# A state-space layer beside attention: the causal mask once per group, the sigmoid's linear part on ScalarE, chunk-end decays from the middle's, step sums later

## The chip, the cores and the metric

The kernel runs on one core of a Trainium2 chip. A core has a matrix engine (TensorE, in the profile PE for its matmuls and PEld for its weight loads), a vector engine (VectorE, DVE), an engine for functions of one input (ScalarE, ACT), a general engine (GpSimd, POOL) and SyncE (SP), whose queue issues most of the weight loads. Each engine works through its own queue in order; semaphores hold an instruction until its inputs are there. The metric is the device time of one execution in microseconds, the median of several runs.

## The reference

Input `x` has 256 positions of 1024 numbers. Two layers follow each other, then a norm over the 1024 columns.

The first layer projects the normed `x` into eight parts: a gate `z`, the state-space inputs `xs`, `B`, `C`, the step sizes `dt`, and `q`, `k`, `v`, a gate rank and an output gate for gated linear attention.

The state-space half: a causal convolution of width 4 and silu over `xs`, `B`, `C`; then for 16 heads in two groups, with `a_cs` the running sum of `dt * a`,

```python
decay_ij = jnp.exp(jnp.where(causal, a_cs_i - a_cs_j, -jnp.inf))
cb = jnp.einsum('bcign,bcjgn->bcgij', c_c, b_c)          # one per group
y_diag = einsum(cb * decay_ij, x * dt)                   # one per head
```

The linear attention half, in chunks of 64 positions, with `gcs` the running sum of `log_sigmoid(gate) / 16` within a chunk and `ref` its value in the chunk's middle (position 32):

```python
scores = einsum(q * exp(gcs - ref), k * exp(ref - gcs))  # within a chunk, causal
chunk_kv = einsum(k * exp(g_last - gcs), v)              # what a chunk leaves behind
o_inter = einsum(q * exp(gcs), prev_states)              # what a chunk takes over
```

Both halves are normed, gated and projected back. The second layer is softmax attention over 16 heads with its own projections.

## The kernel before

The sequence has 256 positions, so a tile of 128 partitions by 256 columns holds one block of 128 features for all positions. Weights come in pieces of 416 or 512 KB through SP's queue; `split` (L73 to L78) makes a high part of each piece on ScalarE (L76) and the rest on VectorE (L77), and every projection is three matmuls per 128 input features: high by high, high by rest, rest by high (`mm3`, L166). In the profile `pb` is the PSUM tile of the projections by block of features, `pa` of those by position, `h_b`, `l_b`, `h_a`, `l_a` the two parts of their weights.

TensorE's order is written out by the program itself. A planner (L129 to L153) keeps a clock of its own, `clock["now"]`, to which each matmul adds a price (L155 to L160: 106.7 ns for the 128 x 256 matmul of a projection). Small tasks are generators: each does a step and then yields a number of ns, and `due()` runs after each `mm3` the steps whose time has come. The numbers are in `DL` (L26 to L28). So a larger number puts more projection matmuls ahead of a step. VectorE, ScalarE and GpSimd are not ordered by hand except at the very start: the scheduler of the language takes, engine by engine, what is ready in its own model of time, earlier lines of the program first. The resulting queues are fixed in the program.

The main loop (L610 to L625) goes through `ORDER_A`: blocks 8 and 9 (`B`, `C`), 10 to 17 (`q` and `k`), 0 to 7 (`xs`) and the position-wise projections `a2` to `a4`, mixed. Around it run these tasks:

- `co_first` (L360): from the first projections the step sizes `dt` and `dta`, a chain of some dozen small VectorE instructions that ends at L388; then after `gt` the transposed gate rank, after `ac` the matmuls `acp` (L397, running sums of `dta`), after `act` their transpose and, in two steps `lg`, the gate products (`lg`, L412). From each, `gab` = |g + b| on ScalarE (L416) and `gmn` = min(g + b, 0) on VectorE (L417); then Exp and Ln over `gab`, which need two tables, their difference (L422) and the running sum `gcs` within each chunk (L423).
- `co_conv` (L435), one per block 0 to 9: `pad`, a scaling on ScalarE, three VectorE instructions `cu` (L444), a Tanh and the product `xs` or `bc` (L448).
- `co_cb` (L457): the products `cb` of `C` and `B`, one per group, copied to `cbT` (L465).
- `co_pair` (L468), one per block 0 to 7, two heads: the transpose `xtp` of `xs`, its product with `dt` (`xdt`), the decays `e` (Relu and Exp on ScalarE, L481 to L485), the causal mask on them by GpSimd (L487, one select per head over two 128 x 128 parts), the product with `cbT` (L489) and the matmuls `yp`.
- `co_gla_qk` (L508): from `gcs` the four decay tiles `e1` to `e4` and their products with `q` or `k` (L517 to L528), and the tiles `qs`, `ks` (L533 to L536). `co_gla_pair` (L541) uses them in the score matmuls `gs` and the outputs `go`.

After these come the second half of the first layer (`pc`), the attention layer (`pv`, `pp`, `as`, `ptp`, `ao`) and the last projection (`pf`).

Of the kernel before, what the change touches and what calls it, by code (L numbers as in the profile page):

```python
# [9 lines left out]
F32 = mybir.dt.float32  # L10
F32R = mybir.dt.float32r
AF = mybir.ActivationFunctionType
ALU = mybir.AluOpType
AX = mybir.AxisListType

P = 128
T = 256
# [5 lines left out]
NWARM = 20  # L23
AHEAD = 4

DL = {"rb": 1300, "gt": 1500, "ac": 7300, "act": 2600, "lg": 2150, "ln": 2250, "cb": 12400,  # L26
      "pair0": 11900, "pair1": 9700, "gla0": 650, "glagap": 3650, "gla1": 3350, "gla2": 8700, "r2": 10000,
      "turn": 4150, "rb1": 4000, "at0": 2600, "at2": 5000, "at1": 3700, "at3": 1800, "gqk": 250}  # L28

# [6 lines left out]
C_CW, C_CB, C_GB, C_DS, C_GN = 24, 64, 74, 78, 86  # L36
# [8 lines left out]
def trunk(ctx, tc, xT_d, x_d, cst_d, mat_d, gw2_d, fn_d, wa_d, wb_d, wc_d, wv_d, wp_d, wf_d, out_d):  # L45
    nc = tc.nc
    V, S, G, TE = nc.vector, nc.scalar, nc.gpsimd, nc.tensor

    cpool = ctx.enter_context(tc.tile_pool(name="consts", bufs=1))
# [5 lines left out]
    sm = ctx.enter_context(tc.tile_pool(name="sm", bufs=2))  # L55
# [125 lines left out]
    cst = cpool.tile([P, C_N], F32, name="cst")  # L181
# [178 lines left out]
    def co_first(ps):  # L360
        rcol = env["rcol"]
        V.tensor_scalar(rhalf, rcol, 0.5, None, op0=ALU.mult)
        V.tensor_tensor(rsq, rcol, rcol, op=ALU.mult)
        V.tensor_scalar(rsv, rsq, 1.0 / P, None, op0=ALU.mult)
        V.tensor_scalar(rsh, rsq, 0.5, None, op0=ALU.mult)
        V.tensor_scalar(cwh, cst[:, C_CW:C_CW + 50], 0.5, None, op0=ALU.mult)
        S.activation(ea, cst[:, C_AL:C_AL + 16], AF.Exp)
        for c in range(2):
            for tt in range(2):
                tm_evac(c, tt, ps[c][tt])  # L370
        env["a1"] = True
        yield DL["rb"]
        S.activation(rb, row_bcast([rcol[:, tt:tt + 1] for tt in range(2)], "rbp")[:, 0:T], AF.Copy)
        env["rb"] = True

        V.scalar_tensor_tensor(na, dtr, -1.0, dtr, op0=ALU.mult, op1=ALU.min)
        S.activation(se, na, AF.Exp)
        V.tensor_scalar(sd, se, 2.0, None, op0=ALU.add)
        V.reciprocal(sd, sd)
        V.tensor_tensor(s1, se, sd, op=ALU.mult)  # L380
        V.tensor_tensor(s2, s1, s1, op=ALU.mult)
        V.tensor_scalar(sp, s2, 1.0 / 17, None, op0=ALU.mult)
        for q_ in (15, 13, 11, 9, 7, 5, 3):
            V.scalar_tensor_tensor(sp, sp, 1.0 / q_, s2, op0=ALU.add, op1=ALU.mult)
        V.scalar_tensor_tensor(sp, sp, 1.0, s1, op0=ALU.add, op1=ALU.mult)
        V.tensor_scalar(mx, dtr, 0.0, None, op0=ALU.max)
        V.scalar_tensor_tensor(dt, sp, 2.0, mx, op0=ALU.mult, op1=ALU.add)
        V.scalar_tensor_tensor(dta, dt, -1.0, ea[:, None, :].to_broadcast([P, 2, 16]), op0=ALU.mult, op1=ALU.mult)  # L388
        yield DL["gt"]
        gtp = pm("gtp")  # L390
        for tt in range(2):
            tr(gtp[0:16, tt * P:tt * P + P], glr[:, tt, :])
        V.tensor_copy(glT, gtp[0:16, 0:T])
        yield DL["ac"]
        acp = pm("acp")
        for tt in range(2):
            mm(acp[0:16, tt * P:tt * P + P], dta[:, tt, :], tri[tt])  # L397
        V.tensor_copy(acT, acp[0:16, 0:T])
        S.activation(ahl[0:16, :], acp[0:16, 0:T], AF.Copy)
        V.tensor_sub(ahl[32:48, :], acT, ahl[0:16, :].bitcast(F32))  # L400
        V.tensor_copy(sel, mat[:, M_SEL:M_SEL + 16])
        yield DL["act"]
        act = pm("act")
        for tt in range(2):
            TE.transpose(act[:, 16 * tt:16 * tt + 16], acT[:, tt * P:tt * P + P], ident[0:16, 0:16])
        V.tensor_copy(acs, act[:, 0:32].rearrange("p (a b) -> p a b", a=2))

        for b2 in range(2):
            lg = pm(f"lg{b2}")
            for j in range(2):  # L410
                b = 2 * b2 + j
                mm(lg[:, j * T:j * T + T], gw2[:, b * P:b * P + P], glT)  # L412
            for j in range(2):
                b = 2 * b2 + j
                gbc = cst[:, C_GB + b:C_GB + b + 1]
                S.activation(gab[:, b, :], lg[:, j * T:j * T + T], AF.Abs, bias=gbc)  # L416
                V.tensor_scalar(gmn[:, b, :], lg[:, j * T:j * T + T], gbc, 0.0, op0=ALU.add, op1=ALU.min)  # L417
            yield DL["lg"]
        S.activation(gab, gab, AF.Exp, scale=-1.0)
        S.activation(gab, gab, AF.Ln, bias=1.0)  # L420
        yield DL["ln"]
        V.tensor_sub(gmn, gmn, gab)  # L422
        V.tensor_tensor_scan(flat(gcs), flat(scanm), flat(gmn), 0.0, op0=ALU.mult, op1=ALU.add)  # L423
        env["gcs"] = True


# [30 lines left out]
    def co_cb():  # L457
        yield DL["cb"]
        for g in range(2):
            r = slice(64 * g, 64 * g + 64)  # L460
            ps = pm(f"cb{g}")
            mm(ps[:, 0:T], bc[r, 0, 0:P], bc[r, 1, :])
            mm(ps[:, T:T + P], bc[r, 0, P:T], bc[r, 1, P:T])
            sb = big.tile([P, 3 * P], F32, name=f"cbT{g}", tag=f"cbT{g}")
            S.activation(sb, ps[:, 0:3 * P], AF.Copy)  # L465
            cbT.append(sb)

    def co_pair(blk):  # L468
        yield DL["pair0"]
        tp = pm(f"xtp{blk}")  # L470
        for tt in range(2):
            tr(tp[:, tt * P:tt * P + P], xs[:, blk, tt * P:tt * P + P])
        xdt = tmp.tile([P, 2, 2, 64], F32, name=f"xdt{blk}", tag="t1c")
        V.tensor_tensor(xdt, tp[:, 0:T].rearrange("p (a b c) -> p a b c", a=2, b=2),
                        dt[:, :, 2 * blk:2 * blk + 2][:, :, :, None].to_broadcast([P, 2, 2, 64]), op=ALU.mult)
        e = tmp.tile([P, 2, 3, P], F32, name=f"e{blk}", tag="t3")
        for j in range(2):
            h = 2 * blk + j
            ab = pm(f"ab{h}")
            mm(ab[:, 0:T], sel[:, h:h + 1].to_broadcast([P, P]), ahl)  # L480
            S.activation(e[:, j, 0:2, :].rearrange("p a b -> p (a b)"), ab[:, 0:T], AF.Relu, scale=-1.0,  # L481
                         bias=acs[:, 0, h:h + 1])
            S.activation(e[:, j, 2, :], ab[:, P:T], AF.Relu, scale=-1.0, bias=acs[:, 1, h:h + 1])
        ef = e.rearrange("p a b c -> p (a b c)")
        S.activation(ef, ef, AF.Exp, scale=-1.0)  # L485
        for j in range(2):
            G.affine_select(out=e[:, j, 0:3:2, :], in_=e[:, j, 0:3:2, :], pattern=[[0, 2], [1, P]],  # L487
                            compare_op=ALU.is_ge, fill=0.0, base=0, channel_multiplier=-1)
        V.tensor_tensor(e, e, cbT[blk // 4].rearrange("p (a b) -> p a b", a=3)[:, None, :, :].to_broadcast([P, 2, 3, P]),  # L489
                        op=ALU.mult)  # L490
        yield DL["pair1"]
        yp = pm(f"yp{blk}")
        rows = [slice(64 * j, 64 * j + 64) for j in range(2)]
        for j, r in enumerate(rows):
            mm(yp[r, 0:T], xdt[:, 0, j, :], e[:, j, 0:2, :].rearrange("p a b -> p (a b)"), True, False)
        for j, r in enumerate(rows):
            mm(yp[r, P:T], xdt[:, 1, j, :], e[:, j, 2, :], False, True)
        V.scalar_tensor_tensor(y[:, blk, :], xs[:, blk, :], cst[:, C_DS + blk:C_DS + blk + 1], yp[:, 0:T],
                               op0=ALU.mult, op1=ALU.add)
# [8 lines left out]
    def co_gla_qk():  # L508
# [5 lines left out]
        e3 = big.tile([P, 16, 64], F32, name="e3", tag="s3")  # L514
        e4 = big.tile([P, 16, 64], F32, name="e4", tag="s4")
        dl = cpool.tile([P, 4, 4], F32, name="dl")
        V.tensor_tensor(e2, gcs, gcs[:, :, 32:33].to_broadcast(full), op=ALU.subtract)  # L517
        V.tensor_tensor(e4, gcs[:, :, 63:64].to_broadcast(full), gcs, op=ALU.subtract)
        S.activation(e1, e2, AF.Exp, scale=1.0 / 16)
        S.activation(e2, e2, AF.Exp, scale=-1.0 / 16)  # L520
        S.activation(e3, gcs, AF.Exp, scale=1.0 / 16)
        S.activation(e4, e4, AF.Exp, scale=1.0 / 16)
        S.activation(dl.rearrange("p a b -> p (a b)"), gcs[:, :, 63], AF.Exp, scale=1.0 / 16)
        env["gla"] = (e1, e2, e3, e4, dl)
        V.scalar_tensor_tensor(e1, qf, 0.125, e1, op0=ALU.mult, op1=ALU.mult)
        V.scalar_tensor_tensor(e3, qf, 0.125, e3, op0=ALU.mult, op1=ALU.mult)
        V.tensor_tensor(e2, kf, e2, op=ALU.mult)
        V.tensor_tensor(e4, kf, e4, op=ALU.mult)  # L528
        qs = big.tile([P, 4, 2, 64], F32, name="qs", tag="qs")
        ks = big.tile([P, 4, 2, 64], F32, name="ks", tag="ks")  # L530
        e3v = e3.rearrange("p (a c) d -> p a c d", a=4)
# [417 lines left out]
```

## Time and profile before

| | |
|---|---|
| median of 3 runs | 344.76 us (344.56 to 344.84) |
| profiled execution, its own time | 343.5 us |
| its span, first to last instruction | 341.8 us |
| busy: TensorE, VectorE, ScalarE, GpSimd | 330.9, 260.6, 235.0, 38.1 us |
| granted TensorE clock, mean | 0.996 of full |

Every row below is from that one profiled execution; times are us from the span's start unless they are marked ns. Columns of the views, from the left:

- waits: the instruction that stood, what released it, us in total, how many times, the longest
- chain: start, length, engine, what (rows overlap less than the instructions do, since each counts from the end of the one before)
- stretches: the stretch, its length, then for each engine named in the group's line its busy time and, in brackets, its instructions; then the granted clock, the share of the DMA engines and GB/s
- time line: start, length, engine, line, operation, what it writes and reads, shapes, count; in square brackets the idle time of its engine just before, and who ended it
- groups: line, engine, operation, tiles, shapes, count; busy us and mean ns of one; idle us before and what ended it

### The profile page before, as it was taken

How to read it: one execution, taken by the hardware profiler on the slowest of the kernel's cores; microseconds unless marked ns; L12 is line 12 of the kernel's file. 1: busy time of each engine (PE TensorE's matmuls, PEld its weight loads, DVE VectorE, ACT ScalarE, POOL GpSimd, SP SyncE). 2: the span in 40 equal slices, each digit the busy share in tenths (PEclk: the TensorE clock that was granted, in tenths of full speed). 3: DMA queues.
4: the chain of work that ended last, by engine and by line, in shares of the span. 5: the costliest groups of instructions: out<-in, count | busy, mean ns of one | idle time of the engine just before them, and what ended most of it. 6: DMA issues, size and time to landing. Idle time of an engine off the chain costs nothing.

```text
span 341.8 us, 5949 instructions
## 1 busy us (share of the span) xinstructions
PE 330.9 (97%) x2160; PEld 294.2 (86%) x2160; DVE 260.6 (76%) x538; ACT 235.0 (69%) x495; POOL 38.1 (11%) x56
## 2 busy tenths in 40 slices
PE   7999799999999999999999999999999999999992
PEld 7999789999888899999888888888888888888782
DVE  3978987998999767889975756557869689596552
ACT  4858669897567847768442766565797886987531
POOL 1000000223311241434300000000000000000000
PEclk9999999999999999999999999999999999999998
DMA  7995772454157834621687436637607327070003
GB/s 221 333 334 185 239 257 61 110 166 150 51 151 233 297 122 153 221 81 46 196 281 256 145 123 231 226 132 256 185 5 245 125 99 261 12 245 3 0 2 123
DMA packets 18094, 56.07 MB, mean 164 GB/s; under 512 B 2048, under 2 KB 5120, under 8 KB 17936
## 3 DMA queue, kind: packets, MB, share of 16 engines
q1 hardware_dynamic: 17344, 53.53, 48.3%
q10 hardware_dynamic: 720, 2.16, 1.8%
q8 instruction: 17, 0.28, 0.3%
q14 instruction: 13, 0.11, 0.1%
HBM read 54.63 MB, written 1.05 MB: 163 GB/s over the span
## 4 chain that ended last, share of the span: by engine, by line
PE 67%; DVE 5%; issue 2%; POOL 0%; ACT 0%; POOLq 0%
PE pp L159 20%; PE pc L159 13%; PE pb L159 7%; PE pv L159 6%; PE pa L159 6%; PE pf L159 4%; PE ao L159 2%; PE go L159 2%; PE as L159 2%; PE gs L159 2%; PE ptp L163 2%; DVE cu L444 1%; PE yp L159 1%; DVE l_a L77 1%; PE obt L163 1%
## 5 line engine op out<-in xcount | busy, mean ns | idle before, releaser
L159 PE MATMUL pb<-hh,h_b 128*128 128x256 f32 x416 | 76.9, 286 | 0.0
L159 PE MATMUL pp<-h,h_p 128*128 128x512 f32 x192 | 67.6, 402 | 0.0
L159 PEld LDWEIGHTS pb<-hh,h_b 128*128 128x128 f32 x416 | 64.6, 191 | 1.4 <-issue 0.9
L159 PE MATMUL pb<-hh,l_b 128*128 128x256 f32 x208 | 58.7, 282 | 0.0
L159 PE MATMUL pp<-h,l_p 128*128 128x256 f32 x192 | 49.9, 280 | 0.0
L159 PE MATMUL pa<-h_a,hh 128*128 128x416 f32 x160 | 42.6, 357 | 1.0 <-ACT h_a L76 1.0
L159 PEld LDWEIGHTS pp<-h,h_p 128*128 128x128 f32 x192 | 34.5, 188 | 7.0 <-issue 0.5
L159 PEld LDWEIGHTS pb<-hh,l_b 128*128 128x128 f32 x208 | 39.7, 191 | 0.0
L159 PEld LDWEIGHTS pp<-h,l_p 128*128 128x128 f32 x192 | 36.2, 189 | 2.2
L77 DVE TENSOR_TENSOR l_p<-r_p,h_p 128x1024 fp32r<-128x1024 f32 x24 | 29.2, 1222 | 8.9 <-ACT h_p L76 8.0
L77 DVE TENSOR_TENSOR l_b<-r_b,h_b 128x1024 fp32r<-128x1024 f32 x26 | 31.5, 1212 | 1.7 <-ACT h_b L76 1.5
L76 ACT ACTIVATE h_b<-r_b 128x1024 fp32r<-128x1024 f32 x26 | 27.1, 1060 | 7.1 <-DMA r_b<-in_wb 6.5
L159 PEld LDWEIGHTS pa<-h_a,hh 128*128 128x128 f32 x160 | 29.8, 188 | 2.5 <-ACT h_a L76 1.3
L76 ACT ACTIVATE h_p<-r_p 128x1024 fp32r<-128x1024 f32 x24 | 25.1, 1056 | 1.7 <-PE pv L159 1.6
L159 PE MATMUL pa<-l_a,hh 128*128 128x416 f32 x80 | 24.9, 351 | 0.0
L77 DVE TENSOR_TENSOR l_c<-r_c,h_c 128x1024 fp32r<-128x1024 f32 x16 | 19.9, 1251 | 5.4 <-ACT h_c L76 5.4
L76 ACT ACTIVATE h_c<-r_c 128x1024 fp32r<-128x1024 f32 x16 | 16.9, 1055 | 10.1 <-DMA r_c<-in_wc 8.8
L77 DVE TENSOR_TENSOR l_a<-r_a,h_a 128x832 fp32r<-128x832 f32 (+1 forms) x21 | 20.6, 986 | 2.5 <-ACT h_a L76 2.5
L76 ACT ACTIVATE h_a<-r_a 128x832 fp32r<-128x832 f32 (+1 forms) x21 | 18.1, 862 | 6.1 <-DMA r_a<-in_wa 5.9
L159 PE MATMUL pv<-h_v,h 128*128 128x512 f32 x64 | 20.1, 391 | 0.0
L487 POOL TENSOR_SCALAR_AFFINE_SELECT e<-e 128x256 f32<-128x256 f32 x16 | 11.6, 749 | 73.3 <-ACT e L485 59.4
L764 ACT ACTIVATE pt<-pt,nm 128x128 f32<-128x128 f32 (+1 forms) x32 | 14.2, 444 | 5.6 <-DVE nm L762 5.6
(234 smaller groups left out, 715.3 us busy)
## 6 DMA issues: line engine op xcount, KB each, us to landing
r_b<-in_wb SPq DMA_DIRECT2D x26, 512.0 KB, 4.2
r_p<-in_wp SPq DMA_DIRECT2D x24, 512.0 KB, 4.2
r_c<-in_wc SPq DMA_DIRECT2D x16, 512.0 KB, 4.0
r_a<-in_wa SPq DMA_DIRECT2D x19, 416.0 KB, 3.9
r_v<-in_wv SPq DMA_DIRECT2D x8, 512.0 KB, 4.4
r_f<-in_wf SPq DMA_DIRECT2D x8, 512.0 KB, 3.9
xT<-in_xT SPq DMA_DIRECT2D x8, 128.0 KB, 4.8
x<-in_x ACTq DMA_DIRECT2D x1, 1024.0 KB, 6.1
```

The lines of the kernel that those rows point to most:

```text
L76: S.activation(hi, raw, AF.Copy)
L77: V.tensor_sub(lo, raw, hi.bitcast(F32))
L159: TE.matmul(out, lhsT, rhs, start=start, stop=stop)
L163: TE.transpose(out, in_, ident)
L444: V.scalar_tensor_tensor(u, pd[:, 1 + i:1 + i + T], w(i), u, op0=ALU.mult, op1=ALU.add)
L487: G.affine_select(out=e[:, j, 0:3:2, :], in_=e[:, j, 0:3:2, :], pattern=[[0, 2], [1, P]], compare_op=ALU.is_ge, fill=0.0, base=0, channel_ ...
L764: S.activation(pt[:, cs], pt[:, cs], AF.Exp, scale=-1.0, bias=nm[:, tt:tt + 1], accum_out=sme[:, tt:tt + 1])
```

## The change

`ac` grows from 7300 to 10000, so `acp` and what hangs on it in `co_first` stand later in TensorE's order. The four `min(g + b, 0)` on VectorE become four `Relu(-(g + b))` on ScalarE, with the sign turned in the two instructions that follow. The mask goes from the decays of each head to `cbT`, once per group. In `co_gla_qk` the tiles `e3` and `e4` are no longer made by Exp from their own differences: `e3` is the finished `e1` times `exp(ref)`, `e4` the finished `e2` times `exp(g_last - ref)`, one factor per chunk and feature, and only for the three chunks each that are read.

```diff
-DL = {"rb": 1300, "gt": 1500, "ac": 7300, "act": 2600, ...
+DL = {"rb": 1300, "gt": 1500, "ac": 10000, "act": 2600, ...
...
+        gbn = sm.tile([P, 4], F32, name="gbn", tag="gbn", bufs=1)
+        V.tensor_scalar(gbn, cst[:, C_GB:C_GB + 4], -1.0, None, op0=ALU.mult)
...
-                V.tensor_scalar(gmn[:, b, :], lg[:, j * T:j * T + T], gbc, 0.0, op0=ALU.add, op1=ALU.min)
+                S.activation(gmn[:, b, :], lg[:, j * T:j * T + T], AF.Relu, scale=-1.0, bias=gbn[:, b:b + 1])
...
-        V.tensor_sub(gmn, gmn, gab)
-        V.tensor_tensor_scan(flat(gcs), flat(scanm), flat(gmn), 0.0, op0=ALU.mult, op1=ALU.add)
+        V.tensor_tensor(gmn, gmn, gab, op=ALU.add)
+        V.tensor_tensor_scan(flat(gcs), flat(scanm), flat(gmn), 0.0, op0=ALU.mult, op1=ALU.subtract)
...
             S.activation(sb, ps[:, 0:3 * P], AF.Copy)
+            diag = sb.rearrange("p (a b) -> p a b", a=3)[:, 0:3:2, :]
+            G.affine_select(out=diag, in_=diag, pattern=[[0, 2], [1, P]],
+                            compare_op=ALU.is_ge, fill=0.0, base=0, channel_multiplier=-1)
...
-        for j in range(2):
-            G.affine_select(out=e[:, j, 0:3:2, :], in_=e[:, j, 0:3:2, :], pattern=[[0, 2], [1, P]],
-                            compare_op=ALU.is_ge, fill=0.0, base=0, channel_multiplier=-1)
...
+        V.tensor_tensor(fl(dr), gcs[:, :, 63], gcs[:, :, 32], op=ALU.subtract)
         V.tensor_tensor(e2, gcs, gcs[:, :, 32:33].to_broadcast(full), op=ALU.subtract)
-        V.tensor_tensor(e4, gcs[:, :, 63:64].to_broadcast(full), gcs, op=ALU.subtract)
         S.activation(e1, e2, AF.Exp, scale=1.0 / 16)
         S.activation(e2, e2, AF.Exp, scale=-1.0 / 16)
-        S.activation(e3, gcs, AF.Exp, scale=1.0 / 16)
-        S.activation(e4, e4, AF.Exp, scale=1.0 / 16)
-        S.activation(dl.rearrange("p a b -> p (a b)"), gcs[:, :, 63], AF.Exp, scale=1.0 / 16)
+        S.activation(fl(dl), gcs[:, :, 63], AF.Exp, scale=1.0 / 16)
+        S.activation(fl(dm), gcs[:, :, 32], AF.Exp, scale=1.0 / 16)
+        S.activation(fl(dr), fl(dr), AF.Exp, scale=1.0 / 16)
         V.scalar_tensor_tensor(e1, qf, 0.125, e1, op0=ALU.mult, op1=ALU.mult)
-        V.scalar_tensor_tensor(e3, qf, 0.125, e3, op0=ALU.mult, op1=ALU.mult)
         V.tensor_tensor(e2, kf, e2, op=ALU.mult)
-        V.tensor_tensor(e4, kf, e4, op=ALU.mult)
+        V.tensor_tensor(f4(e3)[:, :, 1:4, :], f4(e1)[:, :, 1:4, :], dm[:, :, 1:4, None].to_broadcast([P, 4, 3, 64]),
+                        op=ALU.mult)
+        V.tensor_tensor(f4(e4)[:, :, 0:3, :], f4(e2)[:, :, 0:3, :], dr[:, :, 0:3, None].to_broadcast([P, 4, 3, 64]),
+                        op=ALU.mult)
```

## Rows read from the trace of the kernel before

**Rows 1.** The page: span, and busy us of each engine

```profile
span 341.8 us, 5949 instructions
...
PE 330.9 (97%) x2160; PEld 294.2 (86%) x2160; DVE 260.6 (76%) x538; ACT 235.0 (69%) x495; POOL 38.1 (11%) x56
```

**Rows 2.** TensorE's waits (PE), whole span

```profile
PE acp L159 <- DVE dta L388: 2.1, 1, 2.1
PE warmp L177 <- DVE mhalf L203: 1.3, 1, 1.3
PE pa L159 <- ACT h_a L76: 1.0, 1, 1.0
PE xtp L163 <- DVE xs L448: 0.2, 1, 0.2
```

**Rows 3.** Chain of waits, 85 us to the end

```profile
91.87 0.33 DVE ks L535
...
98.68 0.35 DVE xs L448
...
99.07 0.44 PE xtp L163 x2
...
99.74 2.15 PE pb L159 x18
...
114.59 1.64 PE gs L159 x20
```

**Rows 4.** Stretch 58.40 to 99.10 us: PE, PEld, DVE, ACT, POOL

```profile
58.40:99.10 40.70, 40.49 (x311) 37.46 (x309) 38.37 (x64) 31.47 (x59) 11.12 (x14) 1.00 0.39 112
```

**Rows 5.** VectorE's waits, 58 to 100 us

```profile
DVE e L489 <- POOL e L487: 2.3, 3, 1.0
```

**Rows 6.** Time line around `acp` and `act`

```profile
39.79 0.17 DVE L388 SCALAR_TENSOR_TENSOR dta<-dt,ea 128x32 f32<-128x32 f32 x1
...
40.02 0.61 PE L159 MATMUL acp<-mat,dta 128*16 128x128 f32 x4 [2.11 <-DVE dta L388]
...
43.99 0.29 PE L405 MATMUL act<-mat,acT 16*128 16x16 f32 x2
```

**Rows 7.** Stretch 40.50 to 43.98 us, instructions of `pb`: PE, PEld, DVE, ACT

```profile
40.50:43.98 3.48, 3.42 (x27) 3.30 (x27) 0.42 (x1) 0.00 (x0) 1.00 0.84 226
```

**Rows 8.** Groups by form, 40 to 115 us

```profile
L487 POOL TENSOR_SCALAR_AFFINE_SELECT e<-e 128x256 f32<-128x256 f32 x14 | 10.9, 797 | 62.9 <-ACT e L485 49.0 <-DVE pad L439 7.2 <-issue 6.7
...
L489 DVE TENSOR_TENSOR e<-e,cbT 128x768 f32<-128x768 f32 x7 | 6.7, 952 | 3.0 <-POOL e L487 3.0
...
L417 DVE TENSOR_SCALAR gmn<-lg,cst 128x256 f32<-128x256 f32 x4 | 1.9, 479 | 0.5 <-ACT gab L416 0.5
L416 ACT ACTIVATE gab<-lg,cst 128x256 f32<-128x256 f32 x4 | 1.9, 476 | 1.1 <-DVE gmn L417 0.9
...
L518 DVE TENSOR_TENSOR e<-gcs 128x1024 f32<-128x1024 f32 x1 | 1.2, 1211 | 0.0
...
L521 ACT ACTIVATE e<-gcs 128x1024 f32<-128x1024 f32 x1 | 1.1, 1062 | 0.0
```

**Rows 9.** Time line around `cbT` and block 1's `xs` and `xtp`

```profile
49.89 0.87 ACT L465 ACTIVATE cbT<-cb 128x384 f32<-128x384 f32 x2 [0.37 <-PE cb L159]
...
63.20 0.42 DVE L448 SCALAR_TENSOR_TENSOR xs<-cth,cu 128x256 f32<-128x256 f32 x1
64.28 0.96 DVE L489 TENSOR_TENSOR e<-e,cbT 128x768 f32<-128x768 f32 x1 [0.66 <-POOL e L487]
...
65.83 0.38 PE L163 MATMUL xtp<-mat,xs 128*128 128x128 f32 x2
```

**Rows 10.** Time line of ScalarE around Ln

```profile
52.23 1.28 ACT L420 ACT_TABLE_LOAD   x1
53.53 1.06 ACT L420 ACTIVATE gab<-gab 128x1024 f32<-128x1024 f32 x1
...
58.64 1.28 ACT L521 ACT_TABLE_LOAD   x1
```

More of the change, by code (lines that the diff above doesn't have):

```diff
@@ L24 @@
 AHEAD = 4
-DL = {"rb": 1300, "gt": 1500, "ac": 7300, "act": 2600, "lg": 2150, "ln": 2250, "cb": 12400,
+DL = {"rb": 1300, "gt": 1500, "ac": 10000, "act": 2600, "lg": 2150, "ln": 2250, "cb": 12400,
       "pair0": 11900, "pair1": 9700, "gla0": 650, "glagap": 3650, "gla1": 3350, "gla2": 8700, "r2": 10000,
@@ L516, in co_gla_qk @@
         dl = cpool.tile([P, 4, 4], F32, name="dl")
+        dr = cpool.tile([P, 4, 4], F32, name="dr")
+        dm = cpool.tile([P, 4, 4], F32, name="dm")
+        fl = lambda a: a.rearrange("p a b -> p (a b)")
+        f4 = lambda a: a.rearrange("p (a c) d -> p a c d", a=4)
+        V.tensor_tensor(fl(dr), gcs[:, :, 63], gcs[:, :, 32], op=ALU.subtract)
         V.tensor_tensor(e2, gcs, gcs[:, :, 32:33].to_broadcast(full), op=ALU.subtract)
-        V.tensor_tensor(e4, gcs[:, :, 63:64].to_broadcast(full), gcs, op=ALU.subtract)
         S.activation(e1, e2, AF.Exp, scale=1.0 / 16)
         S.activation(e2, e2, AF.Exp, scale=-1.0 / 16)
-        S.activation(e3, gcs, AF.Exp, scale=1.0 / 16)
-        S.activation(e4, e4, AF.Exp, scale=1.0 / 16)
-        S.activation(dl.rearrange("p a b -> p (a b)"), gcs[:, :, 63], AF.Exp, scale=1.0 / 16)
+        S.activation(fl(dl), gcs[:, :, 63], AF.Exp, scale=1.0 / 16)
+        S.activation(fl(dm), gcs[:, :, 32], AF.Exp, scale=1.0 / 16)
+        S.activation(fl(dr), fl(dr), AF.Exp, scale=1.0 / 16)
         env["gla"] = (e1, e2, e3, e4, dl)
         V.scalar_tensor_tensor(e1, qf, 0.125, e1, op0=ALU.mult, op1=ALU.mult)
-        V.scalar_tensor_tensor(e3, qf, 0.125, e3, op0=ALU.mult, op1=ALU.mult)
         V.tensor_tensor(e2, kf, e2, op=ALU.mult)
-        V.tensor_tensor(e4, kf, e4, op=ALU.mult)
+        V.tensor_tensor(f4(e3)[:, :, 1:4, :], f4(e1)[:, :, 1:4, :], dm[:, :, 1:4, None].to_broadcast([P, 4, 3, 64]),
+                        op=ALU.mult)
+        V.tensor_tensor(f4(e4)[:, :, 0:3, :], f4(e2)[:, :, 0:3, :], dr[:, :, 0:3, None].to_broadcast([P, 4, 3, 64]),
+                        op=ALU.mult)
         qs = big.tile([P, 4, 2, 64], F32, name="qs", tag="qs")
```

## The prediction

> **What bounds the kernel now.** I read the page's busy times first, then TensorE's waits, then the chain, then the stretches that these pointed at. The page gives TensorE 330.9 of 341.8 us [rows 1]. A modelled busy time alone proves little, so the second view decides: all the time in which TensorE stood waiting is four rows, 4.6 us together [rows 2]. Two of them (1.3 and 1.0 us) lie at the very start, before the first weights are split, and no edit touches them. The third is the one to look at: 2.11 us in which the matmuls `acp`, the running sums of the step sizes, wait for `dta` from VectorE. The fourth is 0.2 us before an `xtp`, a transpose that waits for a convolution block `xs`. So the kernel is bound by the order and amount of TensorE's work, and only what removes or adds a TensorE wait moves the end.
>
> That fourth row is small but tells of a second limit. The chain of waits enters TensorE at 99.07 us, at that `xtp`, straight from VectorE [rows 3]; ahead of it VectorE was busy 38.37 of 40.70 us from 58.40 to 99.10 [rows 4], and the missing 2.3 us are three waits of the decay product (L489) for GpSimd's mask [rows 5]. So around 99 us VectorE delivers just in time: if TensorE comes earlier, VectorE must come earlier too, or the gain is handed back there.
>
> The sum below is made against the profiled execution, 343.5 us with a span of 341.8; the median of the runs shown is 344.76, which is 1.26 more. I add that at the end.
>
> **The change, part by part.**
>
> *The step sums later (`ac` 7300 to 10000).* TensorE's order is written out by the planner. It lets a due step in after each group of three matmuls, which it charges 3 x 106.7 = 320 ns (L160). 2700 ns more are 8.4, thus 9 groups: 27 matmuls of the projection are put ahead of `acp`. In the trace 18 of them take 2.15 us [rows 3], 27 take 3.2 us; the stretch between `acp` and the next step, `act`, holds just 27, from 40.02 + 0.61 = 40.6 to 43.99 us [rows 6, 7]. Without its wait TensorE would have begun `acp` at 40.02 - 2.11 = 37.91; now it comes there at 37.91 + 3.2 = 41.1. `dta` ends at 39.79 + 0.17 = 39.96 [rows 6], and nothing ahead of it on VectorE is changed except one tiny negation (`gbn`, at the 0.17 us of `dta`). That leaves 1.0 us, so I take the whole wait as gone: -2.11 us. Bounds: 0 (if `dta` comes later by more than 1.0 + 2.1 us) to -2.11. No DMA is moved: splits and weight loads are issued by the projection blocks, whose order stays. What hangs on `acp` (its transpose, the gate products, the gate's scan) comes 3.2 - 2.1 = 1.1 us later on the clock.
>
> *Relu on ScalarE for min on VectorE.* Four VectorE instructions of 0.48 us go, four ScalarE ones of the same shape as the Abs (0.48 us) come [rows 8]: 1.9 us from one engine to the other, off TensorE. Abs and min took turns on one bank of PSUM, with waits for each other in either direction; both now stand in one queue. ScalarE waits for `gbn`, which needs only a constant.
> The Trainium skill ("ScalarE: Activation LUTs", Rules for kernel authors) says to give relu, min and add to VectorE instead. For these fp32 blocks out of PSUM the trace does not bear it out: 479 ns on VectorE, 476 on ScalarE [rows 8]. Were the rule right, the swap would cost ScalarE more than VectorE wins, and still no TensorE time.
>
> *Scan.* The subtraction before the scan becomes an addition and the scan adds the opposite sign: same shapes, 0 either way.
>
> *Chunk-end decays from the middle's.* VectorE loses one difference and two full products of 1024 columns, three instructions of 1.21 us (L518; L526 and L528 like it): -3.63 us. It gains two products of 768 columns; the nearest row is the 768-column decay product with a broadcast operand, 0.95 us [rows 8], so +1.9 (bounds: three quarters of 1.21, thus 0.91, and 1.21 each), and a 16-column difference, +0.17. ScalarE loses two Exp of 1.06 [rows 8] and gains two of 16 columns, which cannot be longer than the 0.48 of 256 columns; with the four Relu its balance is between -0.2 and +0.8 us, beside 235 us of work in a span of 342 [rows 1]. In series the new products come later, since `e3` waits for the finished `e1`. That is hidden: the last of the old ones, `ks`, ends at 92.2 and the first score matmul `gs` that reads them comes at 114.6 [rows 3], 22 us later. What the new products may wait for is ScalarE's small Exp; behind them in VectorE's queue stand convolutions. In the trace VectorE's only waits between 58 and 100 us were for GpSimd [rows 5], none for the old Exp, so I price this at 0 and keep the three-wait total of 2.3 us as its upper end.
>
> *Mask once per group.* GpSimd loses 16 selects of about 0.8 us [rows 8] and gets two. The first product that needs the masked `cbT` starts at 64.28; the copy is done at 50.76 [rows 9]. Two selects fit there many times, so the added wait costs nothing. What goes is VectorE's 2.3 us of standing before L489 [rows 5] and up to two selects of latency ahead of each `yp`.
>
> *VectorE's ledger up to 99 us*, which decides whether the gain lives: -3.63 + 1.9 + 0.17 - 2.3 = -3.9 us. To serve TensorE 2.11 us earlier, and without today's 0.24, it must gain 2.35. That leaves 1.5 us, and the 1.9 us of min removed before 52 us are not counted.
>
> **The sum:** 343.5 - 2.1 = 341.4 for the profiled execution; with 1.26 added, 342.6 us. Behind the `xtp` at 99 us TensorE has no wait at all [rows 2], so I let the rest shift as a whole.
>
> **Rivals.**
>
> *Part of the gain comes back at the second `xtp`.* The gate chain (Exp, Ln, scan) comes 1.1 us later on the clock. Convolution block 1 shares its queues; its `xs` ends at 63.62 and its `xtp` starts at 65.83 [rows 9], which becomes 63.72. If the block is late by the same 1.1 us, TensorE stands 64.72 - 63.72 = 1.0 us, and the gain is 1.1: 343.7. For it: VectorE is without a gap there. Against it: VectorE has 1.9 us less to do ahead of it.
>
> *VectorE keeps its clock.* The scheduler re-plans VectorE's queue for the whole program; if the saved time is filled by weight splits that could have waited, `xs` still ends at 99.03 [rows 3] and TensorE waits there 0.24 + 2.11 us. The profile then shows an `acp` without a wait and the same span: 344.8. The same end comes if the sums are moved but `dta` comes later too, so that the change does not do what it says.
>
> *Slower: the logarithm lands ahead of block 1's Tanh.* The ScalarE queue swaps its tables for Ln and back: a load of 1.28, Ln itself about 1.06 like the other 1024-column functions, another load of 1.28 [rows 8, 10]: 3.62 us in which no Tanh can run. Today it begins at 52.23, ahead of the block's work. Moved against the blocks by 3.2 us of TensorE work it may stand right ahead of the Tanh. Then `xs` of block 1 ends at 63.62 + 3.62 = 67.24 where TensorE is ready at 63.72; it waits 3.52, less the 2.11 won: +1.4 us, 346.2. It decides once this `xs` ends later than 65.83, today's start of its `xtp`. For it: both loads are needed in any order. Against it: the Exp of L521, 1.06 us of that queue, is gone.
> The same page of the Trainium skill (What ACT_TABLE_LOAD costs) adds a drain of 1.38 us to each load. The trace shows none: Ln's load starts at 52.23 and Ln at 53.53 [rows 10]. By the page this rival would end near 349.0.
>
> **How the numbers follow.** About 0.2%, 0.7 us, is what a measurement of this kernel can tell from no change. The forecast, 342.6, gets 0.58, with its own range of 341.9 to 343.3. Part back: 0.16, around 343.7, nearly all of it still faster by more than 0.7. VectorE keeps its clock: 0.12, no change. Slower: 0.14, from 345.5 to 346.5 or beyond, other orders of the queues that end late among them. Faster 0.73, the same 0.13, slower 0.14. The range reaches from 341.8, where no wait but those of the start is left and a little noise is added, over no change to 345.2, and leaves out most of the slower case.
>
> **What would show it.** Right: TensorE's waits hold no `acp` row and no `xtp` row above 0.3 us; `dta` still ends near 40 us and `acp` starts near 41.1; VectorE shows no wait for GpSimd before L489; `gs` starts near 112.4; the span is near 339.7. Wrong: an `acp` wait that is left (`dta` moved too), a wait of 1 us or more at an `xtp` (block 1 or the one at 97 us), or a `yp` or `gs` that waits for a product behind ScalarE's Exp. The forecast fails if any of these waits passes 1.4 us, for then less than 0.7 us of the gain remains.

## The result, and the profile after

The changed kernel takes 340.93 us (median of 4, 340.65 to 341.28) against 344.66 us of the kernel before: a ratio of 0.9895, 95% interval 0.9873 to 0.9917, so 3.7 us (2.9 to 4.4) faster. The forecast was 342.6 and its range began at 341.8: right in direction, too small by 1.7 us.

The page of the changed kernel, span and busy times, answers to [rows 1]:

```profile
span 338.9 us, 5921 instructions
...
PE 331.0 (98%) x2160; PEld 295.0 (87%) x2160; DVE 257.1 (76%) x535; ACT 234.8 (69%) x499; POOL 29.7 (9%) x42
```

TensorE has the same work, 331.0 against 330.9 us, in 2.9 us less of span. All its waits, against the four of [rows 2]:

```profile
PE warmp L177 <- DVE mhalf L203: 1.3, 1, 1.3
```

Only the unavoidable one at the start is left. Those for `acp` and for the `xtp` are gone, as forecast; the 1.0 us for the first weights is a matter of the single execution (the traces below show between 0 and 0.9 us there). The time line around `acp` answers to [rows 6]:

```profile
39.29 0.17 DVE L388 SCALAR_TENSOR_TENSOR dta<-dt,ea 128x32 f32<-128x32 f32 x1
...
40.57 0.61 PE L159 MATMUL acp<-mat,dta 128*16 128x128 f32 x4
...
44.53 0.29 PE L405 MATMUL act<-mat,acT 16*128 16x16 f32 x2
```

`dta` ends at 39.46 and `acp` starts at 40.57, 1.1 us behind it; 1.0 was forecast. In the chain of waits, `acp` now stands between projection matmuls that follow each other without a gap:

```profile
1.25 4.64 PE warmp L177 x20
...
29.14 11.50 PE pb L159 x96
40.64 0.54 PE acp L159 x4
41.19 3.42 PE pb L159 x27
```

VectorE between 58.40 and 99.10 us ([rows 4]; after the stretch and its length come PE, PEld, DVE, ACT, POOL, then the granted clock), and the 3.3 us behind `acp`, which the experiments come back to:

```profile
58.40:99.10 40.70, 40.70 (x313) 38.02 (x312) 39.75 (x66) 34.35 (x67) 3.21 (x2) 1.00 0.47 136
41.10:44.40 3.30, 3.30 (x28) 3.29 (x27) 2.83 (x6) 2.75 (x5) 0.00 (x0) 1.00 0.92 284
```

VectorE's waits from 58 to 100 us; the three for GpSimd of [rows 5] are gone:

```profile
DVE gs L273 <- ACT gth L272: 0.5, 1, 0.5
DVE xs L450 <- ACT cth L448: 0.2, 1, 0.2
DVE l_b L77 <- ACT h_b L76: 0.2, 1, 0.2
```

The new operations by form, answering to [rows 8]:

```profile
L419 ACT ACTIVATE gmn<-lg,gbn 128x256 f32<-128x256 f32 x4 | 1.9, 474 | 0.0
...
L470 POOL TENSOR_SCALAR_AFFINE_SELECT cbT<-cbT 128x256 f32<-128x256 f32 x2 | 1.2, 628 | 24.9 <-ACT cbT L467 24.9
...
L536 DVE TENSOR_TENSOR e<-e,dm 128x768 f32<-128x768 f32 x1 | 0.9, 950 | 0.0
L538 DVE TENSOR_TENSOR e<-e,dr 128x768 f32<-128x768 f32 x1 | 0.9, 944 | 0.0
```

The Relu takes the 0.47 us of the Abs beside it, the two products 0.95 and 0.94 us (forecast 0.95), the two selects on `cbT` 0.63 us each (the forecast went by the 0.8 us of the selects on the decays).

The two kernels' profiled executions are 343.5 and 340.65 us, 2.85 apart. 2.11 and 0.24 of that are the two waits, and 0.5 stands at the start (the first `pb` comes at 24.88 instead of 25.38 us). So the profiles account for the forecast's sum and for nothing of the additional gain: the medians lie 3.73 apart. What the median of before holds and its profiled execution doesn't is the first question of the experiments.

### The profile page after: what moved, and what is told of

The parts are those of the page before. It is cut to its first block, busy times and chain, and to the rows that moved or that the text cites. A ratio compares the mean times of both kernels' runs of the same rounds, so it can differ in the third digit from the quotient of the medians.

```text
span 338.9 us, 5921 instructions
## 1 busy us (share of the span) xinstructions
PE 331.0 (98%) x2160; PEld 295.0 (87%) x2160; DVE 257.1 (76%) x535; ACT 234.8 (69%) x499; POOL 29.7 (9%) x42
## 4 chain that ended last, share of the span: by engine, by line
PE 96%; issue 2%; DVE 1%; ACT 0%; POOLq 0%; POOL 0%
PE pb L159 22%; PE pp L159 20%; PE pa L159 14%; PE pc L159 13%; PE pv L159 6%; PE pf L159 5%; PE yp L159 2%; PE ao L159 2%; PE go L159 2%; PE as L159 2%; PE gs L159 2%; PE ptp L163 2%; PE warmp L177 1%; PE obt L163 1%; PE lg L159 1%
## 5 line engine op out<-in xcount | busy, mean ns | idle before, releaser
L446 DVE SCALAR_TENSOR_TENSOR cu<-pad,cwh,cu 128x256 f32<-128x256 f32 x30 | 14.4, 481 | 1.3 <-ACT cu L444 1.2
```

Source lines behind the costliest of these rows:

```text
L446: V.scalar_tensor_tensor(u, pd[:, 1 + i:1 + i + T], w(i), u, op0=ALU.mult, op1=ALU.add)
```

## The experiments

Every kernel was timed beside the kernel before, in three groups, each on a chip of its own; the median of before was 344.55, 344.59 and 344.86 us there. Theories and rivals are named A to H in the recorded expectations; where a letter comes back in a later run it has the sense that this run's text gives it.

**What a second trace of before shows.** No edit.

> The kernel before once more, for a second trace of it and for what two equal programs differ by. The forecast added 1.26 us to the profiled execution (343.5 against a median of 344.76) as if that were constant. Theory A with waits that vary: an execution near 344.7 shows more TensorE wait than the 4.6 us of the first trace, by about 1.2 us, at acp (its dta stands in VectorE's queue behind weight splits that wait for their loads) or at an xtp. Rival, the start: the additional 1.2 us stands before 26 us, in the waits for the first weights, and the acp wait is again 2.1. Rival, neither: same waits, and the difference lies outside the span. Timed against before: within 0.2%.

Measured: 344.05 (12 executions from 343.21 to 345.65), ratio 0.9995 (0.9977 to 1.0013); the traced execution took 344.73. TensorE's waits are those of [rows 2] but for the start: `acp` 2.1, `xtp` 0.2, no `pa`. The time line of its TensorE:

```profile
39.80 0.61 PE L159 MATMUL acp<-mat,dta 128*16 128x128 f32 x4 [2.09 <-DVE dta L388]
...
45.25 0.29 PE L405 MATMUL act<-mat,acT 16*128 16x16 f32 x2
```

From `acp` to `act` it needs 45.25 - 39.80 = 5.45 us, in the first trace 43.99 - 40.02 = 3.97 [rows 6], for the same 27 matmuls [rows 7]. The stretches show why (the third number from the right is the granted clock):

```profile
40.00:41.00 1.00, 1.00 (x9) 0.78 (x8) 1.00 (x2) 0.30 (x1) 0.00 (x0) 1.00 0.62 152
...
41.02:44.43 3.41, 3.41 (x18) 3.41 (x17) 2.08 (x4) 1.32 (x2) 0.00 (x0) 0.50 0.82 270
44.43:48.00 3.57, 3.57 (x27) 3.04 (x26) 3.35 (x8) 2.46 (x5) 0.00 (x0) 1.00 0.67 247
```

Behind the wait, which ends at 39.80, `acp` and the first projection matmuls still run at full clock. From 41.02 us on, 1.2 us behind the wait's end, the granted clock is 0.50 for 3.41 us, that is 1.2 instead of 2.4 GHz, and 18 matmuls go through where 28 do in the first trace, in nearly the same stretch at full clock:

```profile
41.10:44.40 3.30, 3.30 (x28) 3.17 (x27) 3.24 (x6) 2.08 (x3) 0.00 (x0) 1.00 0.90 272
```

So neither longer waits nor the start nor the time outside the span: a fourth cause that no theory had. It costs 5.45 - 3.97 = 1.48 us. Of the 52 executions of before beside the experiments, 14 took 343.0 to 343.9 us and 38 took 344.1 or more (of the twelve here, six each); the first profile, at 343.5, was of the shorter kind. The mean granted clock that is recorded with each execution fits: 0.995 to 0.997 in the 14, 0.991 to 0.994 in 37 of the 38 (the one of 344.14 us has 0.997), and 3.41 us at half clock are 0.005 of such a span. It is a hint and no proof, since this mean also counts what falls after the last matmul, where it costs nothing (in the first trace the clock is 0.50 from 340 us on, and the last matmul ends at 335.5).

**The wait filled with work.** This tells a clock that falls because TensorE stands from one that falls at this place for another reason.

```diff
-        acp = pm("acp")
+        acp = pm("acp"); [TE.matmul(acp[:, T:2 * T], hhi[:, 0, 0:P], hhi[:, 0, :], start=True, stop=True) for _ in range(16)]
```

> The kernel before with 16 matmuls of no use (128x256, into the unused half of acp's own bank) just ahead of acp, so that TensorE works through the 1.9 us that it otherwise stands; the queues of the other engines are unchanged in order. Seen so far: in two of three traces with the acp wait of 2.1 us the granted clock is at its lower level for 3.41 us right behind it, and these executions are about 1.2 us longer than the one without. Theory D (clock): it is standing still that lets the clock fall; with the wait filled the clock stays at the upper level in every execution and the time is that of the faster executions of before, 343.2 to 343.7 median, 0.8 to 1.3 us under the median of before, though the 2.1 us are as lost as ever. Rival E (the lower clock comes from something else at that place, such as acp's narrow matmuls or the loads): the clock still falls in most executions and the median stays within 0.4 us of before. Rival F (the start): the two groups of times come from the first weights, and the median stays as before.

Measured: 343.43, ratio 0.9972 (0.9960 to 0.9983); nine of ten executions took 343.0 to 343.7, the tenth 344.51. The mean granted clock is 0.995 to 0.998 in all ten, so the tenth is not late by the clock. The 16 matmuls fill the wait to 0.19 us, and the clock behind stays up:

```profile
37.62 2.08 PE L395 MATMUL acp<-hh 128*128 128x256 f32 x16
39.89 0.61 PE L159 MATMUL acp<-mat,dta 128*16 128x128 f32 x4 [0.19 <-DVE dta L388]
```

```profile
41.10:44.40 3.30, 3.30 (x28) 3.14 (x27) 3.18 (x6) 2.03 (x4) 0.00 (x0) 1.00 0.85 256
```

`acp` comes no earlier (39.89) and nothing else is changed, yet about 1.2 us of the median go: theory D, with rivals E and F out. What the matmuls of no use do is to leave only the shorter kind of execution; the 2.1 us themselves stay lost.

**Half the wait.** `ac` at 8300 in the changed kernel.

```diff
-DL = {"rb": 1300, "gt": 1500, "ac": 10000, "act": 2600, ...
+DL = {"rb": 1300, "gt": 1500, "ac": 8300, "act": 2600, ...
```

> The changed kernel with the delay ahead of acp at 8300: 6 groups of three matmuls, 2.15 us, earlier than in the changed kernel, where dta is 1.1 us ahead of acp. So acp should wait about 1.0 us. If the cost of a wait is its length alone: 1.0 us above the changed kernel, 341.9 to 342.1. Theory D with a clock that falls after any wait: another 1.2 to 1.7 us in most executions, 343.1 to 343.7, and the clock at its lower level behind acp in the trace. Theory D with a clock that falls only after a wait long enough: as by length alone, with the clock at its upper level.

Measured: 342.03, ratio 0.9929 (0.9913 to 0.9944), all five executions from 341.81 to 342.32. TensorE's waits, and the stretch behind `acp`:

```profile
PE warmp L177 <- DVE mhalf L203: 1.3, 1, 1.3
PE acp L159 <- DVE dta L388: 1.0, 1, 1.0
PE pa L159 <- ACT h_a L76: 0.9, 1, 0.9
```

```profile
41.10:44.40 3.30, 3.30 (x27) 3.10 (x26) 2.71 (x5) 2.27 (x3) 0.00 (x0) 1.00 0.95 292
```

The wait is 1.0 us, the kernel 1.1 us slower than the changed one, and the clock stays at the upper level in this trace: here the wait cost its length.

**The early sums in the changed kernel.** `ac` back to 7300, the three other edits kept.

```diff
-DL = {"rb": 1300, "gt": 1500, "ac": 10000, "act": 2600, ...
+DL = {"rb": 1300, "gt": 1500, "ac": 7300, "act": 2600, ...
```

> The changed kernel with the delay ahead of acp set back from 10000 to 7300, all else as changed. Theory A: the acp wait is back with 2.0 to 2.6 us, the xtp wait stays at 0, so it is slower than the changed kernel by 2.0 to 2.6 us and ahead of before by 0.2 us plus what differs from run to run. Theory B: equal to before, 344.7. Theory C: ahead of before by 1.3 to 1.7 us, with an acp wait of 2.1.

Measured: 344.34, ratio 0.9993 (0.9976 to 1.0010). As theory B has it, equal to before, and 3.4 us above the changed kernel: 2.1 us of wait, and in the traced execution (344.86) the granted clock is 0.50 from 41.4 to 44.8 us.

```profile
PE acp L159 <- DVE dta L388: 2.1, 1, 2.1
PE warmp L177 <- DVE mhalf L203: 1.3, 1, 1.3
```

```profile
41.40:44.75 3.35, 3.35 (x18) 3.35 (x17) 1.95 (x4) 1.24 (x3) 0.00 (x0) 0.50 0.82 291
```

The `xtp` wait is gone with the lightened VectorE, but that is 0.2 us. Without the later sums nothing is gained.

**The later sums alone.** The kernel before with `ac` at 10000; run twice.

```diff
-DL = {"rb": 1300, "gt": 1500, "ac": 7300, "act": 2600, ...
+DL = {"rb": 1300, "gt": 1500, "ac": 10000, "act": 2600, ...
```

> The kernel before with one number changed: the delay ahead of acp is 10000 instead of 7300. Theory A (the forecast's): TensorE's waits decide, and VectorE has no time to spare at 99 us. The acp wait of 2.1 us goes, but VectorE's queue is otherwise unchanged, so most of it comes back as a wait for xs at the xtp of the sixth or seventh block: a wait of 1 to 2.4 us there, and a gain over before of 0 to 1.2 us. Theory B (the later step alone is the change, VectorE's relief is idle time off the path): the whole gain of 3.7 us, near 341.0, and no xtp wait above 0.3 us. Theory C (the relief of VectorE and GpSimd is worth about 1.5 us by itself, the acp wait 2.1): a gain of 2.0 to 2.4 us, no xtp wait above 0.3 us.

> The later step sums alone once more, for a second trace. Its first profiled execution was 341.57, with a gs wait of 1.1 us, though the median was 342.48. If the wait varies with the loads: 1.1 to 2.5 us at gs in this trace, in step with its time. If the wait drops the clock in some executions, as the acp wait did: the clock is at its lower level for 3.41 us behind it and the time is 342.8 or more.

Measured: 342.48 both times, ratios 0.9942 (0.9923 to 0.9961) and 0.9945 (0.9924 to 0.9966): 2.1 to 2.4 us under before, 1.55 above the changed kernel. That is the gain that theory C names, but C also wanted the changed kernel with early sums 1.3 us or more ahead of before, and it was not; A fails for want of an `xtp` wait, and B, which the early sums had borne out, by its time. So none of the three is right for both runs: the other edits are worth 1.55 us behind the later sums and nothing without them. No `xtp` waits at all. `xs` of the block that was late at 99.03 in [rows 3] is done at 94.91, with nothing taken from VectorE; it has been laid ahead of one of the two weight splits `l_a` that stood ahead of it before:

```profile
94.49 0.42 DVE L448 SCALAR_TENSOR_TENSOR xs<-cth,cu 128x256 f32<-128x256 f32 x1
94.83 1.02 DVE L77 TENSOR_TENSOR l_a<-r_a,h_a 128x832 fp32r<-128x832 f32 x1
```

Instead TensorE stands 1.1 us in the first trace and 1.4 us in the second at the first `gs`, a place the forecast held safe. From the time line of the first (ScalarE, VectorE, TensorE):

```profile
109.74 1.06 ACT L76 ACTIVATE h_b<-r_b 128x1024 fp32r<-128x1024 f32 x1 [1.76 <-DMA r_b<-in_wb]
...
110.84 1.23 DVE L77 TENSOR_TENSOR l_b<-r_b,h_b 128x1024 fp32r<-128x1024 f32 x1
...
112.51 0.42 DVE L474 TENSOR_TENSOR xdt<-xtp,dt 128x256 f32<-128x256 f32 x1
...
112.98 0.37 PE L159 MATMUL gs<-e,e 64*128 64x128 f32 x1 [1.13 <-DVE xdt L474]
```

The `gs` matmuls of the second head wait for `xdt` (L474), which reads block 7's transposed `xs` and so frees its bank of PSUM. Ahead of `xdt` in VectorE's queue stands a weight split `l_b`, whose `h_b` stood 1.76 us for its load. In the same trace that load was issued at 106.29 us, after SyncE's queue had stood 3.5 us for the split `l_a` which VectorE began at 105.20. So VectorE was late, but through a load that its earlier split had let out late, not through the arithmetic near the wait. The clock is at its upper level behind this wait in both traces. Three of the twelve executions, 343.5 to 343.7, are about 1.2 us above the rest. No trace caught one; their mean granted clock is 0.991 to 0.993 against 0.995 to 0.998 in the nine, which speaks for a fall of the clock in them, but where it fell is not shown.

**Which of the three edits lightens VectorE enough.** Each alone with the later sums:

```diff
 # later_and_mask: the kernel before, ac at 10000, and
+            G.affine_select(out=diag, in_=diag, ...      (co_cb, once per group)
-            G.affine_select(out=e[:, j, 0:3:2, :], ...   (co_pair, once per head)
 # later_and_decays: the kernel before, ac at 10000, and
-        V.tensor_tensor(e4, gcs[:, :, 63:64].to_broadcast(full), gcs, op=ALU.subtract)
+        V.tensor_tensor(fl(dr), gcs[:, :, 63], gcs[:, :, 32], op=ALU.subtract)
...
 # later_and_relu: the kernel before, ac at 10000, and
-                V.tensor_scalar(gmn[:, b, :], ..., gbc, 0.0, op0=ALU.add, op1=ALU.min)
+                S.activation(gmn[:, b, :], ..., AF.Relu, scale=-1.0, bias=gbn[:, b:b + 1])
...
```

> The kernel before with the later step sums and the mask once per group; min stays on VectorE, the old decays stay. In the kernel with the later sums alone, the first gs waits 1.1 us for VectorE's last xdt, which stands behind a weight split whose load was late. Theory G (any of the three edits lightens VectorE enough to bring its splits, and so the loads, forward): VectorE loses its waits for GpSimd, no gs wait above 0.3 us, 340.8 to 341.3. Rival H (two edits are needed): a gs wait of 0.3 to 0.9 us, 341.3 to 342.2.

> The kernel before with the later step sums and the new decays; mask per head, min on VectorE. Theory G: VectorE has 1.55 us less by its instructions, no gs wait above 0.3 us, 340.8 to 341.3. Rival H: a gs wait of 0.3 to 0.9 us, 341.3 to 342.2.

> The kernel before with the later step sums and Relu on ScalarE; mask per head, old decays. VectorE has 1.9 us less before 52 us and nothing less after. Theory G: if its queue holds that lead up to 110 us, no gs wait; the forecast's ledger did not count on it. Rival H: the lead is lost by 60 us in VectorE's waits for TensorE and ScalarE, so the gs wait stays at 0.8 to 1.3 us and the time at 342.2 to 342.7, as with the later sums alone.

Measured: 341.11 with the mask (ratio 0.9896, 0.9878 to 0.9914), 340.68 with the decays (0.9885, 0.9867 to 0.9903), 342.14 with Relu (0.9934, 0.9914 to 0.9955). The first two have no `gs` wait; with Relu it is 1.2 us. Two of the times lie just under what was expected (340.68 under 340.8, 342.14 under 342.2). The time line with the decays: the two splits go through back to back, and `xdt` waits for its transpose, not for a load.

```profile
107.44 2.36 DVE L77 TENSOR_TENSOR l_b<-r_b,h_b 128x1024 fp32r<-128x1024 f32 x2 [0.17 <-ACT h_b L76]
...
111.37 0.43 DVE L474 TENSOR_TENSOR xdt<-xtp,dt 128x256 f32<-128x256 f32 x1 [0.21 <-PE xtp L163]
...
111.49 0.73 PE L159 MATMUL gs<-e,e 64*128 64x128 f32 x3
```

So mask and decays are each enough, and Relu, whose 1.9 us fall before 52 us, brings nothing to 110 us: theory G's result for two edits, rival H's for the third. Whether an edit helps because VectorE has less to do or because its queue is laid in another order, these runs don't separate. The later sums with the decays alone are as fast as the whole change (340.68 against 340.93; the intervals of the ratios overlap almost entirely).

**One edit undone at a time in the changed kernel.** The mask per head, the old decays, min on VectorE: the same lines as above, the other way round.

```diff
 # mask_per_head: the changed kernel, and
-            G.affine_select(out=diag, in_=diag, ...      (co_cb, once per group)
+            G.affine_select(out=e[:, j, 0:3:2, :], ...   (co_pair, once per head)
 # decays_undone: the changed kernel, and
-        V.tensor_tensor(fl(dr), gcs[:, :, 63], gcs[:, :, 32], op=ALU.subtract)
+        V.tensor_tensor(e4, gcs[:, :, 63:64].to_broadcast(full), gcs, op=ALU.subtract)
...
 # min_on_vector: the changed kernel, and
-                S.activation(gmn[:, b, :], ..., AF.Relu, scale=-1.0, bias=gbn[:, b:b + 1])
+                V.tensor_scalar(gmn[:, b, :], ..., gbc, 0.0, op0=ALU.add, op1=ALU.min)
...
```

> The changed kernel with the causal mask back on the decays of each head by GpSimd, 16 selects, and cbT unmasked. VectorE then waits for GpSimd before some of the decay products again, about 2 us by 99 us. Theory A: by the ledger (3.9 us won, 2.35 needed) 1.5 us remain, less the 2.3 of these waits: the xtp wait comes back with 0 to 0.8 us, slower than the changed kernel by 0 to 0.8 us. Theory B: no difference within 0.2%. Theory C: slower by about 1 us, the GpSimd part of the relief, without a TensorE wait that shows it.

> The changed kernel with the old decays in the linear attention: e3 and e4 from their own differences and Exp, two products of 1024 columns instead of two of 768. VectorE has 1.7 us more to do before 92 us, ScalarE about 1.6 us more. In the kernel with the later sums alone, TensorE waited 1.1 us for VectorE's xdt at the first gs. Theory G (that wait is VectorE's load, and the decays are what lightens it): the gs wait is back with 0.3 to 1.1 us, 341.3 to 342.5. Rival H (the order in which the scheduler lays VectorE's queue decides it, not the load): no wait, within 0.3 us of the changed kernel.

> The changed kernel with the four min back on VectorE instead of Relu on ScalarE. VectorE has 1.9 us more to do before 52 us, ScalarE 1.9 us less. The forecast took this edit as free: within 0.3 us of the changed kernel, no TensorE wait above 0.3 us. Rival G (VectorE's load up to the first gs decides): a gs wait of 0.3 to 1.1 us, up to 1 us slower. Rival: the gate chain gets longer, since Abs and min take turns again, and an xtp or gs waits for it.

Measured: 341.24 (ratio 0.9909, 0.9892 to 0.9927), 341.14 (0.9911, 0.9892 to 0.9931) and 340.81 (0.9893, 0.9876 to 0.9910). With the mask per head the `gs` wait is back with 0.4 us, with the other two there is none; all three times are within 0.3 us of the changed kernel. For the decays this is rival H's result and against theory G as it stood there, since VectorE has more to do and no wait returns. No single one of the three is needed.

## Why the prediction was wrong

**The step that failed is the last line of the sum**: 343.5 - 2.1 = 341.4 "with 1.26 added". The 1.26 us between the profiled execution and the median was taken for something that both kernels share. Most of it belonged to the very wait that the change removes: in most executions of before the 2.11 us of standing are followed by 3.41 us at 1.2 GHz, which cost another 1.48 us. So the term of the wait, put at -2.11 with bounds of 0 to -2.11, was worth 3.59 us in most executions. The profiled execution was one of those without. Without that line, the profiled sum held: 343.5 - 2.1 = 341.4 was to come, 340.65 came. Of the 0.75 us between them 0.5 is the start, which is chance (the first `pb` comes between 24.88 and 25.42 us in the fourteen traces), and 0.24 the `xtp` wait, which the sum had left out. In the medians, 2.11 + 1.48 in the executions where the clock falls, and 0.24 of `xtp`, are 3.8 us against 3.73 measured.

**The `acp` wait gone**: right, in place, size and margin, and right that nothing earlier moves `dta`.

**The second limit at 99 us**: wrong. A wait of 0.24 us at one `xtp` was read as a VectorE that could not come earlier. With the later sums alone, and VectorE's work unchanged, the same `xs` came 4.1 us earlier and no `xtp` waited. Being busy 38.37 of 40.70 us told of work laid into that stretch, some of it splits that could have stood elsewhere; the scheduler laid one of them elsewhere.

**The ledger**: the conclusion that VectorE's relief is needed holds, the place doesn't. It is needed at 112 us, where the forecast looked only at `ks` (22 us early) and not at the bank of PSUM that the `gs` of the second head needs. The relief is worth 342.48 - 340.93 = 1.55 us, of which 1.1 to 1.4 are the seen wait.

**Relu, decays, mask**: the prices were right (0.47, 0.95 and 0.94 us) or on the safe side (a select 0.63 us for about 0.8), Relu as free as forecast (340.81 without it), and no product waited behind ScalarE's Exp between 58 and 100 us.

**The rivals**: none came. Block 1's Tanh goes just ahead of the table load, and its `xs` ends at 54.54 us, long before its `xtp` at 63.11; so neither the part that comes back nor the slower case has a place. From the time line of the changed kernel:

```profile
52.83 0.42 ACT L448 ACTIVATE cth<-cu 128x256 f32<-128x256 f32 x1
...
53.27 1.28 ACT L422 ACT_TABLE_LOAD   x1
...
54.12 0.42 DVE L450 SCALAR_TENSOR_TENSOR xs<-cth,cu 128x256 f32<-128x256 f32 x1
```

What none of the cases held is that a wait may cost more than its length. The Trainium skill has that ("TensorE: Matmul & The Clock Gate", HAM oscillation — how this bites in real kernels): when matmuls stand in a wait, the gate falls back and the next ones start slow; the page shows it for longer waits than this one. The traces agree in kind, at 0.50 for 3.41 us behind 2.09 us of waiting, and differ in the order: the first 1.2 us behind the wait ran at full clock. The forecast had only the one trace of before, where the clock stayed up and nothing spoke of this price.

Open is what decides, from one execution to the next, whether the clock falls after the same 2.1 us.

## What to carry to other kernels

A wait of the matrix engine has two prices: its length, and what the clock takes back afterwards. One trace shows one draw of the second; where the median lies 0.4% from the profiled execution, as here, ask what made the difference before carrying it over. An engine that is busy to the brim just ahead of a small wait isn't yet a limit: look whether what fills it could stand elsewhere, and look for who frees the buffers of the next step.

## What the runs showed of the hardware

- After 2.1 us of waiting TensorE ran at a granted clock of 0.50 for 3.41 us in two of three traces, and not in the third. The fall came not at the wait's end but 1.2 and 1.3 us behind it. After 1.0 us at the same place, and after 1.1, 1.2 and 1.4 us at `gs`, it did not come in the one trace each; four executions of the kernels with the `gs` wait that were not traced (343.5 to 344.5 us, mean granted clock 0.991 to 0.993) may hold one.
- 16 matmuls whose result nobody reads, put into that wait, made the kernel 1.2 us faster (344.59 to 343.43), though the work behind them started no earlier.
- Ten executions with the filled wait: nine within 0.7 us (343.0 to 343.7), one at 344.5; the 16 without beside them: 343.6 to 345.0 in two groups, four below 343.9 and twelve above 344.4.
